# Earlier side pieces, reordered products and low parts made by adding transfers, ahead of one gate of a decoder layer

## The chip, the cores and the metric

The kernel runs on one core of a Trainium2 chip. The metric is device time in microseconds (us), the median of several runs. TensorE (PE) multiplies matrices, VectorE (DVE) and ScalarE (ACT) work elementwise, GpSimd (POOL) and SyncE (SP) here only issue DMA transfers. All data are float32; matrix products take operands in the type float32r.

## The reference

One layer of a hybrid decoder over 512 tokens of width 1024. Only the following parts matter here (`h` is the normalised and modulated input, 512 x 1024; the three gates and all mixer inputs are columns of `h @ w_in`):

```python
y_ssd  = (normed y) @ w_ssd_out          # y from the state-space mixer
y_attn = o @ w_attn_out
y_pool = (_multi_scale_pool(u, w_pool_mix) * pool_scale) @ w_pool_out
g_ssd, g_attn, g_pool = split(sigmoid(gates))
x = x + g1 * ((g_ssd * y_ssd + g_attn * y_attn + g_pool * y_pool) @ w_out)
...
x = x + g2 * (square(relu(h2 @ w_ff1)) @ w_ff2)
```

`_multi_scale_pool` takes running means of `u` over windows of 2, 4, 8 and 16 tokens, subtracts `u`, and multiplies each of the four groups of 256 columns by a 256 x 256 matrix of `w_pool_mix`.

## The kernel before, in words

**Products in three parts.** To keep float32 accuracy each operand is split in a high part (`wh`, `xh`: cast to float32r) and a low part (`wl`, `xl`: the original less the high part). A product is three matmuls (`mm3`, lines L293 to L295): high weights by low input, high by high, low weights by high input.

**Chunks.** Activations lie transposed: 8 tiles of 128 features by 512 tokens (`hh`, `hl` for the high and low part of `h`). A weight matrix is used in chunks of 512 output columns. `gemm_feat` computes one chunk: `wstream` loads its rows in steps of 256 (two tiles, 512 KB, one DMA on SP's queue), `wsplit` casts on ScalarE (`wh`) and subtracts on VectorE (`wl`, L279), and TensorE does 2 x 4 x 3 = 24 matmuls of 128 x 512 per step. A chunk of 1024 rows has four steps. The pool `raws` has four buffers for loaded weights; `wsp` has three for `wh` and three for `wl`, so step n is split when step n-3 has been used.

**Seven products.** Some chunks are computed by `seven_products`, a scheme with seven quarter products in place of eight (168 matmuls of 128 x 256, L811). Four of its weight quarters go in as sums (`N`, and `L` in place; made by VectorE, L793 to L796), three as they are: `a00`, `a01`, `a11`. Four of the products use sums of input tiles, `tq`, which `input_sums` makes once for several chunks, in four pieces (VectorE, L753 to L758, then a split into `txh`, `txl`, `tyh`, `tyl`). The others use the plain `hh`, `hl`. It loads the whole chunk as four DMAs: `rawl`, two tiles into the places L0 and L1, and `raw`, two into `raws`. In the code `a00` comes first, then the two products with `N` (for which `tq` is needed), then `a01`, and so on.

**Side pieces.** Small work of other parts (heads of the state-space mixer, norms, the mixes) is a list `side` of functions. `tick()`, called after each step of a weight stream, takes one piece from the list and issues it behind `edges`, the cast and the subtraction of that step. `rest(n)` puts n empty pieces in the list; `flush()` issues all that are left.

**The region of the change.** In order: the two chunks `pool(0)` and `pool(1)` (`u`, then the windows on VectorE, `pdh` and `pdl`), the gate chunk `gate(GS, 0)` (by `gemm_feat`), the projection `project(a["w_ssd_out"], 8, 0, ...)`, the gate chunk `gate(GS, 1, tq)`, which is the first by `seven_products`, and its projection. Beside these, as side pieces: `mix_weights(n)` loads and splits the mix matrices of two groups into the places L0, N0 (n = 0) or L1, N1 (n = 1); `pool_mix(gi)` does the 12 matmuls of one group (`psmix`), scales the result, splits it (`poolh`, `pooll`) and stores it to DRAM by four POOL transfers (L1146); then the four pieces of `input_sums`. When `pool(0)` begins, seven pieces of the state-space heads are still in the list. They and the pieces of this region are taken in the order in which they were put in, one per step.

**Order and places.** Outside a few hand-ordered parts a scheduler orders the instructions of each engine by priority (`high_priority(offset=AHEAD)` for weights, `SOON` for evacuations) and by when it reckons operands to be ready. Each engine's queue is then worked off in order. 49 blocks of 128 x 512 (`blk`) are given out in turn and taken again when they have been used.

Of the kernel before, what the change touches and what calls it, by code (L numbers as in the profile page):

```python
# [17 lines left out]
P = 128  # L18
# [80 lines left out]
def kernel(ctx: ExitStack, tc: tile.TileContext, a: dict, out: bass.AP, dbg=None):  # L99
# [13 lines left out]
    def uid(s):  # L113
        cnt[0] += 1
        return f"{s}_{cnt[0]}"
# [19 lines left out]
    def blk(name, dt=F32):  # L135
        return sb.take(name, dt)
# [18 lines left out]
    def acc():  # L155
        return psm("acc")
# [114 lines left out]
    def flush():  # L271
        while side:
            side.pop(0)()


    def wsplit(raw, shape):
        wh = wsp.tile(shape, F32R, tag="wh", name=uid("wh"))
        wl = wsp.tile(shape, F32R, tag="wl", name=uid("wl"))
        edges[:] = S.copy(wh, raw), V.tensor_tensor(wl, raw, wh.bitcast(F32), ALU.subtract)  # L279
        return wh, wl  # L280

    def wstream(w, nk, ch, k0=0, ahead=None):
        for kp in range(nk // 2):
            with tc.high_priority(offset=AHEAD if ahead is None else ahead):
                raw = raws.tile([P, 2, T], F32, tag="raw", name=uid("raw"))
                nc.sync.dma_start(raw, w[ch, k0 // 2 + kp])
                wh, wl = wsplit(raw, [P, 2, T])
            for i in range(2):
                yield 2 * kp + i, wh[:, i, :], wl[:, i, :]
            tick()  # L290
# [472 lines left out]

        return tq, [piece(k) for k in range(4)]

    def seven_products(w, ch, xh, xl, tq, last=False):

        L, N, H = [], [], []
        in_b = lambda row, ts: lambda k: (xh[4 * row + k][:, ts], xl[4 * row + k][:, ts])
        in_t = lambda n: lambda k: tuple(t[:, halves[n % 2]] for t in tq[k][n // 2])  # L770
        quarters = lambda t: t.rearrange("p i (n c) -> p (i n) c", n=2)
        lo, hi = ta, tb
        with tc.high_priority(offset=AHEAD):
            for m in range(2):
                L.append(exp.tile([P, 2, T], F32, tag=f"L{m}", name=uid("rawl")))
                H.append(raws.tile([P, 2, T], F32, tag="raw", name=uid("raw")))
                nc.sync.dma_start(L[m], w[ch, m])
                nc.sync.dma_start(H[m], w[ch, 2 + m])

            def parts(srcs):  # L780

                wh = wsp.tile([P, 2, T], F32R, tag="wh", name=uid("wh"))
                wl = wsp.tile([P, 2, T], F32R, tag="wl", name=uid("wl"))
                outs = [(wh, wl)] if len(srcs) == 1 else [(quarters(wh)[:, 2 * m : 2 * m + 2, :], quarters(wl)[:, 2 * m : 2 * m + 2, :]) for m in range(2)]
                for x, (h, l) in zip(srcs, outs):
                    S.copy(h, x)  # L786
                    V.tensor_tensor(l, x, h.bitcast(F32), ALU.subtract)  # L787
                return wh, wl

            a00 = parts([L[m][:, :, lo] for m in range(2)])  # L790
            for m in range(2):
                n = exp.tile([P, 2, T], F32, tag=f"N{m}", name=uid("wsum"))
                V.tensor_tensor(n[:, :, lo], L[m][:, :, hi], H[m][:, :, hi], ALU.add)  # L793
                V.tensor_tensor(L[m][:, :, hi], L[m][:, :, lo], L[m][:, :, hi], ALU.subtract)
                V.tensor_tensor(n[:, :, hi], n[:, :, lo], L[m][:, :, lo], ALU.subtract)
                V.tensor_tensor(L[m][:, :, lo], H[m][:, :, lo], n[:, :, hi], ALU.subtract)  # L796
                N.append(n)

        def pair(p, cols):
            return [tuple(t[:, i, cols] for t in p) for i in range(2)]  # L800

        def quarter(p):
            return [tuple(quarters(t)[:, i, :] for t in p) for i in range(4)]

        def product(ps, k0, ws, b, first=False):
            for k, (wh, wl) in enumerate(ws, k0):
                bh, bl = b(k)
                for j in range(2):
                    o, cs = ps[:, j * 256 : j * 256 + 256], slice(j * P, (j + 1) * P)
                    for n, (x, y) in enumerate(((wh, bl), (wh, bh), (wl, bh))):  # L810
                        mm(o, lhsT=x[:, cs], rhs=y, start=first and k == 0 and j == 0 and n == 0, stop=k == 3 and n == 2, skip_group_check=True)  # L811

        def keep(ps):
            with tc.high_priority(offset=SOON):
                t = blk("keep")
                S.copy(t, ps)
            return t

        def add(j0, ts, x, y):
            with tc.high_priority(offset=SOON):  # L820
                for j in range(2):
                    c = slice(j * 256, j * 256 + 256)
                    V.tensor_tensor(rs[j0 + j][:, ts], x[:, c], y[:, c], ALU.add)
            free(x, y)

        X, Z = acc(), acc()
        product(X, 0, quarter(a00), in_b(0, ta), first=True)
        p1 = keep(X)
        for m in range(2):
            with tc.high_priority(offset=AHEAD):  # L830
                s12 = parts([N[m]])
            product(Z, 2 * m, pair(s12, lo), in_t(0), first=True)
            if m == 1:
                p5 = keep(Z)
            product(X, 2 * m, pair(s12, hi), in_t(1))
            tick()
        u2 = keep(X)
        if last:
            for t, _ in tq:
                free(*t)  # L840
        rs = [blk("r") for _ in range(4)]
        with tc.high_priority(offset=AHEAD):
            a01 = parts([H[m][:, :, lo] for m in range(2)])
        Y = acc()
        product(Y, 0, quarter(a01), in_b(1, ta), first=True)
        add(0, ta, Y, p1)
        for m in range(2):
            with tc.high_priority(offset=AHEAD):
                s43 = parts([L[m]])
            product(X, 2 * m, pair(s43, hi), in_t(2))  # L850
            if m == 1:
                u3 = keep(X)
            product(Z, 2 * m, pair(s43, lo), in_b(1, tb))
            tick()
        add(0, tb, Z, u2)
        add(2, tb, u3, p5)
        with tc.high_priority(offset=AHEAD):
            a11 = parts([H[m][:, :, hi] for m in range(2)])
        product(X, 0, quarter(a11), in_t(3))
        with tc.high_priority(offset=SOON):  # L860
            for j in range(2):
                S.copy(rs[2 + j][:, ta], X[:, j * 256 : j * 256 + 256])
        free(X)
        if last:
            for _, t in tq:
                free(*t)
        return rs
# [4 lines left out]
    def gate(c, ch, tq=None, last=False):  # L872
        if tq is None:
            return evac(gemm_feat(w_in, 8, c + ch, hh, hl), "sg", AF.Sigmoid)
        rs = seven_products(w_in, c + ch, hh, hl, tq, last)
        for r in rs:
            S.activation(r, r, AF.Sigmoid)
        return rs
# [221 lines left out]
    def pool(half):  # L1100
        us = evac(gemm_feat(w_in, 8, U + half, hh, hl), "u")
        for j in range(4):
            gi = 2 * half + j // 2
            u = us[j]
            cur, d = u, 1
            while d < WINDOWS[gi]:
                nx = blk("win")
                V.tensor_copy(nx[:, :d], cur[:, :d])
                V.tensor_tensor(nx[:, d:], cur[:, d:], cur[:, : T - d], ALU.add)
                if cur is not u:  # L1110
                    free(cur)
                cur, d = nx, 2 * d
            V.tensor_tensor(cur[:, : d - 1], cur[:, : d - 1], C("edge")[:, gi * 16 : gi * 16 + d - 1], ALU.mult)
            V.scalar_tensor_tensor(cur, cur, 1.0 / d, u, ALU.mult, ALU.subtract)
            free(u)
            x, y = split(cur, "pd")
            free(cur)
            dh.append(x)
            dl.append(y)
# [41 lines left out]
    def call(f, *args):  # L1161
        side.append(lambda: f(*args))
# [22 lines left out]
    def rest(n):  # L1185
        side.extend([lambda: None] * n)
# [55 lines left out]
    project(a["w_attn_out"], 4, 1, oh, ol, sg, first=True)  # L1242
    show("oT", [h.bitcast(F32) for h in oh + ol])
    tq, sums = input_sums(hh, hl)
    for half in range(2):
        call(mix_weights, half)
        pool(half)
        rest(2)
        call(pool_mix, 2 * half)
        if half == 0:  # L1250
            call(pool_mix, 1)
    side.append(lambda: (pool_mix(3), sums[0]()))
    side.extend(sums[1:])
    sg = gate(GS, 0)
    project(a["w_ssd_out"], 8, 0, yh, yl, sg)
    flush()
    sg = gate(GS, 1, tq)
    project(a["w_ssd_out"], 8, 1, yh, yl, sg)

# [262 lines left out]
```

## Time and profile before

| | |
|---|---|
| median of 3 runs | 1106.65 us (1105.22 to 1106.88) |
| the profiled execution | 1104.65 us |
| its span, first to last instruction | 1102.9 us |
| TensorE busy | 1087.0 us, 99% of the span |
| VectorE busy | 761.6 us, 69% |
| ScalarE busy | 536.9 us, 49% |
| GpSimd busy | 29.2 us, 3% |
| mean granted TensorE clock | 0.995 of full speed |
| DMA traffic | 142.42 MB, mean 129 GB/s |

A row of a group or a tile names the line, the engine, the operation and `out<-in`, then durations in ns; a row of the timeline gives the start and the duration in us, and in square brackets how long the engine was idle before, and what ended that. A row of a stretch gives its length and each engine's busy time, the granted clock, the share of the DMA engines' time, and GB/s. Matmuls overlap in the pipeline, so their durations exceed the distance of their starts.

### The profile page before, as it was taken

What the parts mean: (1) busy time and instruction counts of PE and PEld (TensorE: products, weight loads), DVE (VectorE), ACT (ScalarE), POOL (GpSimd) and SP (SyncE); (2) the same over time, 40 slices, a digit from 0 to 9 for tenths busy, and PEclk for the clock granted to TensorE, in tenths of its full rate; (3) what the DMA queues carried; (4) which work ended last, traced back from release to release, by engine and by line L of the source; (5) the groups of instructions that cost most, each with busy time, mean ns of one, the idle gap of its engine ahead of it and who ended that gap; (6) DMA issues with size and microseconds to landing.
All of it is one profiled execution on the core that took longest, in us unless ns stands there. A gap on an engine that the chain in (4) does not pass through costs nothing.

```text
span 1102.9 us, 15616 instructions
## 1 busy us (share of the span) xinstructions
PE 1087.0 (99%) x6022; PEld 937.8 (85%) x6022; DVE 761.6 (69%) x1441; ACT 536.9 (49%) x877; POOL 29.2 (3%) x58
## 2 busy tenths in 40 slices
PE   8999999999999999999988999999999999999998
PEld 7878888888887888888877899899889989989987
DVE  8955746683777956678777557476797587687664
ACT  8965864643545942835425245363344334335330
POOL 0000000000000000000110200000000000000000
PEclk9999999999999999999998999999999999999999
DMA  9723143555644342223534542560224134133032
GB/s 346 296 96 100 65 162 123 176 169 182 203 151 156 102 134 99 93 77 96 191 114 132 172 155 71 178 229 1 77 58 136 64 108 134 56 116 135 20 115 77
DMA packets 49230, 142.42 MB, mean 129 GB/s; under 512 B 5874, under 2 KB 6642, under 8 KB 49156
## 3 DMA queue, kind: packets, MB, share of 16 engines
q1 hardware_dynamic: 43088, 126.08, 34.5%
q0 software_dynamic: 5344, 14.16, 4.2%
q10 hardware_dynamic: 724, 1.18, 0.3%
q8 instruction: 47, 0.77, 0.3%
q14 instruction: 27, 0.22, 0.1%
HBM read 135.08 MB, written 6.32 MB: 128 GB/s over the span
## 4 chain that ended last, share of the span: by engine, by line
PE 79%; issue 16%; DVE 2%; DMA 1%; POOL 1%; ACT 0%; SPq 0%; POOLq 0%; DVEq 0%; ACTq 0%
PE psacc L293 18%; PE psacc L295 18%; PE psacc L294 18%; PE psacc L811 16%; PE psacc L533 4%; PE psS L612 1%; PE pso L728 1%; PE pso L726 1%; POOL pool L1146 1%; PE psqT L591 0%; PE pskT L596 0%; PE pspT L709 0%; DMA xT<-in_x_dram 0%; DMA pool<-pooll 0%; POOL M L1044 0%
## 5 line engine op out<-in xcount | busy, mean ns | idle before, releaser
L279 DVE TENSOR_TENSOR wl<-raw,wh 128x1024 fp32r<-128x1024 f32 x128 | 156.2, 1221 | 138.3 <-ACT wh L279 132.8
L279 ACT CAST wh<-raw 128x1024 fp32r<-128x1024 f32 x128 | 134.2, 1049 | 208.8 <-PE psacc L294 118.6
L293 PE MATMUL psacc<-hl,wh 128*128 128x512 f32 x320 | 128.8, 403 | 0.2 <-ACT pT L710 0.2
L294 PE MATMUL psacc<-hh,wh 128*128 128x512 f32 x320 | 124.6, 390 | 0.0
L295 PE MATMUL psacc<-hh,wl 128*128 128x512 f32 x320 | 124.5, 390 | 0.0
L293 PE MATMUL psacc<-al,wh 128*128 128x512 f32 (+1 forms) x260 | 100.4, 386 | 0.0
L294 PE MATMUL psacc<-ah,wh 128*128 128x512 f32 (+1 forms) x260 | 100.4, 386 | 0.0
L295 PE MATMUL psacc<-ah,wl 128*128 128x512 f32 (+1 forms) x260 | 100.3, 386 | 0.0
L293 PE MATMUL psacc<-wl,rh 128*128 128x512 f32 x192 | 77.4, 403 | 0.0
L295 PE MATMUL psacc<-wh,rl 128*128 128x512 f32 x192 | 75.2, 392 | 0.0
L294 PE MATMUL psacc<-wh,rh 128*128 128x512 f32 x192 | 75.2, 392 | 0.0
L293 PEld LDWEIGHTS psacc<-hl,wh 128*128 128x128 f32 x320 | 60.1, 188 | 13.4 <-issue 1.2
L294 PEld LDWEIGHTS psacc<-hh,wh 128*128 128x128 f32 x320 | 60.2, 188 | 13.3 <-issue 1.4
L295 PEld LDWEIGHTS psacc<-hh,wl 128*128 128x128 f32 x320 | 60.1, 188 | 12.9
L787 DVE TENSOR_TENSOR wl<-rawl,wh 128x512 fp32r<-128x512 f32 (+1 forms) x36 | 33.7, 954 | 35.6 <-ACT wh L786 35.6
L1441 DVE SCALAR_TENSOR_TENSOR xr<-psacc,modv,xr 128x512 f32<-128x512 f32 (+1 forms) x65 | 44.7, 738 | 18.7 <-PE psacc L295 18.7
L295 PEld LDWEIGHTS psacc<-ah,wl 128*128 128x128 f32 x260 | 48.8, 188 | 9.9
L293 PEld LDWEIGHTS psacc<-al,wh 128*128 128x128 f32 x260 | 48.9, 188 | 9.7
L294 PEld LDWEIGHTS psacc<-ah,wh 128*128 128x128 f32 x260 | 48.9, 188 | 9.6
L786 ACT CAST wh<-rawl 128x512 fp32r<-128x512 f32 (+1 forms) x36 | 29.2, 833 | 51.3 <-PE psacc L294 28.7
L786 ACT CAST wh<-wsum 128x1024 fp32r<-128x1024 f32 x18 | 19.0, 1053 | 72.0 <-PE psacc L294 69.5
L811 PE MATMUL psacc<-txl,wh 128*128 128x256 f32 x144 | 42.0, 292 | 4.4 <-DVE txl L321 4.4
(423 smaller groups left out, 2746.5 us busy)
## 6 DMA issues: line engine op xcount, KB each, us to landing
raw<-in_w_in_dram SPq DMA_DIRECT2D x74, 512.0 KB, 3.6
raw<-in_w_ff_dram SPq DMA_DIRECT2D x52, 512.0 KB, 3.8
wa<-in_w_ada_dram SPq DMA_DIRECT2D x64, 256.0 KB, 3.5
wada<-in_w_ada_dram SPq DMA_DIRECT2D x14, 512.0 KB, 7.8
rawl<-in_w_ff_dram SPq DMA_DIRECT2D x12, 512.0 KB, 3.5
wst<-in_w_in_dram SPq DMA_DIRECT2D x16, 256.0 KB, 7.8
M<-prow POOLq DMA_DIRECT2D x16, 256.0 KB, 3.7
raw<-in_w_ssd_out_dram SPq DMA_DIRECT2D x8, 512.0 KB, 3.6
```

What stands on the lines that cost most here:

```text
L279: edges[:] = S.copy(wh, raw), V.tensor_tensor(wl, raw, wh.bitcast(F32), ALU.subtract)
L293: mm(ps, lhsT=wh, rhs=xl, start=first, stop=False)
L294: mm(ps, lhsT=wh, rhs=xh, start=False, stop=False)
L295: mm(ps, lhsT=wl, rhs=xh, start=False, stop=last)
L533: mm(ps[j], lhsT=t[:, j, :], rhs=w, start=first, stop=last)
L612: mm(so[b], lhsT=qT[:, b * P : (b + 1) * P], rhs=kT[:, (b + 1) * P - n : (b + 1) * P], start=True, stop=True)
L726: mm(od, lhsT=vs[kb][:, hs], rhs=pT[b // 2][:, cs : cs + P], start=(b == 0), stop=False, skip_group_check=True)
L728: mm(ov[:, b, :], lhsT=vs[b][:, hs], rhs=pT[0][:, b * P : (b + 1) * P], start=False, stop=(gi == 2 and b == 3), skip_group_check=True)
L786: S.copy(h, x)
L787: V.tensor_tensor(l, x, h.bitcast(F32), ALU.subtract)
L811: mm(o, lhsT=x[:, cs], rhs=y, start=first and k == 0 and j == 0 and n == 0, stop=k == 3 and n == 2, skip_group_check=True)
L1441: V.scalar_tensor_tensor(xT[d][:, ts], p[:, : ts.stop - ts.start], modv[:, 3, d : d + 1], xT[d][:, ts], ALU.mult, ALU.add)
```

## The change

Three edits, all in the region above.

1. The pieces: no `rest(2)`. `pool(0)` and `pool(1)` follow each other with only `mix_weights(0)` put in between; the four mixes go in the list ahead of `gate(GS, 0)`, the second with `mix_weights(1)`; the four input sums behind them, each a piece of its own.
2. In `gate(GS, 1)` the product of `a01` with the plain input (`first_quarter`) is done behind that of `a00`, ahead of the products with `N` and `tq`.
3. In the twelve steps of `pool(1)`, `gate(GS, 0)` and the first projection, `wl` is made another way: ScalarE writes minus `wh` into it, and a transfer issued by GpSimd adds the weights from DRAM to it. VectorE's subtraction falls away.

```diff
+    def wsplit_add(raw, src):
+
+        wh = wsp.tile([P, 2, T], F32R, tag="wh", name=uid("wh"))
+        wl = wsp.tile([P, 2, T], F32R, tag="wl", name=uid("wl"))
+        S.copy(wh, raw)
+        edges[0] = S.mul(wl, wh.bitcast(F32), -1.0)
+        nc.gpsimd.dma_start(wl, src, accum_op=ALU.add)
+        return wh, wl
+
...
-                wh, wl = wsplit(raw, [P, 2, T])
+                if st.get("adds"):
+                    wh, wl = wsplit_add(raw, w[ch, k0 // 2 + kp])
+                else:
+                    wh, wl = wsplit(raw, [P, 2, T])
...
-    def seven_products(w, ch, xh, xl, tq, last=False):
+    def seven_products(w, ch, xh, xl, tq, last=False, sums_late=False):
...
         X, Z = acc(), acc()
         product(X, 0, quarter(a00), in_b(0, ta), first=True)
         p1 = keep(X)
+
+        def first_quarter():
+            rs.extend(blk("r") for _ in range(4))
+            with tc.high_priority(offset=AHEAD):
+                a01 = parts([H[m][:, :, lo] for m in range(2)])
+            Y = acc()
+            product(Y, 0, quarter(a01), in_b(1, ta), first=True)
+            add(0, ta, Y, p1)
+
+        rs = []
+        if sums_late:
+            first_quarter()
         for m in range(2):
...
-        rs = [blk("r") for _ in range(4)]
-        with tc.high_priority(offset=AHEAD):
-            a01 = parts([H[m][:, :, lo] for m in range(2)])
-        Y = acc()
-        product(Y, 0, quarter(a01), in_b(1, ta), first=True)
-        add(0, ta, Y, p1)
+        if not sums_late:
+            first_quarter()
...
-        rs = seven_products(w_in, c + ch, hh, hl, tq, last)
+        rs = seven_products(w_in, c + ch, hh, hl, tq, last, c == GS)
...
     tq, sums = input_sums(hh, hl)
-    for half in range(2):
-        call(mix_weights, half)
-        pool(half)
-        rest(2)
-        call(pool_mix, 2 * half)
-        if half == 0:
-            call(pool_mix, 1)
-    side.append(lambda: (pool_mix(3), sums[0]()))
-    side.extend(sums[1:])
+
+    pool(0)
+    call(mix_weights, 0)
+    st["adds"] = True
+    pool(1)
+    call(pool_mix, 0)
+    side.append(lambda: (mix_weights(1), pool_mix(1)))
+    call(pool_mix, 2)
+    call(pool_mix, 3)
+    side.extend(sums)
     sg = gate(GS, 0)
     project(a["w_ssd_out"], 8, 0, yh, yl, sg)
     flush()
+    st["adds"] = False
     sg = gate(GS, 1, tq)
     project(a["w_ssd_out"], 8, 1, yh, yl, sg)
```

## The prediction

> **What bounds the kernel now.** I read the page first, then the waits of TensorE over the whole run, then stretches of the region that the change touches, then single instructions there.
>
> ```profile
> span 1102.9 us, 15616 instructions
> PE 1087.0 (99%) x6022; PEld 937.8 (85%) x6022; DVE 761.6 (69%) x1441; ACT 536.9 (49%) x877; POOL 29.2 (3%) x58
> PE psacc L811 <- DVE txl L321: 4.4, 2, 3.0
> PE psacc L811 <- ACT wh L786: 3.5, 2, 3.0
> PE psacc L811 <- DVE wl L787: 1.1, 2, 0.7
> ```
>
> The first two lines are the page's head: TensorE (PE) is busy for 1087.0 of 1102.9 us, so nothing that another engine does costs time unless TensorE waits for it. The last three are its largest waits in the whole run: total, times, longest. All stand at L811, the products of `seven_products`, and together they are 9.0 us. The question is whether they lie at one place.
>
> ```profile
> core 0: us, PE busy (x) PEld busy (x) DVE busy (x) ACT busy (x) POOL busy (x), PEclk, DMA share, GB/s
> 493.80:515.60 21.80, 21.80 (x105) 18.12 (x104) 18.64 (x40) 11.97 (x17) 0.00 (x0) 1.00 0.37 117
> 515.60:542.72 27.12, 27.12 (x122) 22.44 (x121) 23.11 (x49) 13.36 (x19) 2.17 (x4) 1.00 0.43 137
> 542.72:569.85 27.13, 26.99 (x119) 22.04 (x118) 17.63 (x28) 6.79 (x10) 4.43 (x9) 1.00 0.32 117
> 569.85:604.43 34.58, 25.52 (x170) 23.92 (x169) 26.12 (x46) 15.94 (x24) 4.69 (x9) 0.85 0.47 152
> 626.38:646.70 20.32, 20.32 (x169) 20.20 (x169) 13.62 (x20) 10.57 (x16) 2.11 (x4) 1.00 0.60 183
> ...
> 569.85:575.15 5.30, 2.33 (x19) 2.10 (x18) 3.60 (x7) 1.81 (x3) 2.02 (x4) 1.00 0.96 316
> 575.15:585.67 10.52, 8.87 (x38) 8.08 (x38) 10.41 (x20) 3.91 (x6) 0.00 (x0) 0.52 0.11 42
> 585.67:604.43 18.76, 14.31 (x115) 13.74 (x115) 12.10 (x20) 10.21 (x15) 2.67 (x5) 1.00 0.54 168
> ```
>
> These are stretches with TensorE's busy time after the comma. The first three are, roughly, `pool(1)`, the first gate chunk with two pool mixes, and the first projection with the other two: TensorE has no hole. The fourth is the first gate made by `seven_products`: 34.58 us. The fifth is the next such gate, with as many products (168 matmuls of L811): 20.32 us. So the first one loses 34.58 - 20.32 = 14.26 us, of which 34.58 - 25.52 = 9.06 is idle. The other 5.2 are the clock: between 575.15 and 585.67 it was granted at 0.52 of full speed.
>
> Why it is late:
>
> ```profile
> 569.84 21.19 SPq L777 DMA_DIRECT2D rawl<-in_w_in_dram  x3
> 573.83 1.29 DVE L753 TENSOR_TENSOR tq<-hh,hl 128x512 f32<-128x512 f32 x2 [1.69 <-DMA pool<-pooll]
> 574.48 0.62 ACT L786 CAST wh<-rawl 128x512 fp32r<-128x512 f32 x1 [3.21 <-DMA rawl<-in_w_in_dram]
> 575.15 0.38 PE L811 MATMUL psacc<-hl,wh 128*128 128x256 f32 x1 [2.97 <-ACT wh L786]
> ...
> 589.35 0.39 PE L811 MATMUL psacc<-txl,wh 128*128 128x256 f32 x1 [1.44 <-DVE txl L321]
> 594.04 0.39 PE L811 MATMUL psacc<-txl,wh 128*128 128x256 f32 x1 [3.00 <-DVE txl L321]
> ...
> L295 PE MATMUL psmix<-pdh,wmN x16: 389/389/390, 531.8 to 569.6; 128*128 128x512 f32 x16
> L321 DVE TENSOR_TENSOR txl<-tq,txh x8: 679/682/691, 570.1 to 819.4; 128x512 fp32r<-128x512 f32 x8
> ```
>
> Two chains, both from the last pool mix. Its matmuls end at 569.6; its weights lie in the place L1 that the second `rawl` load needs, so that load is issued only at 569.84, lands, is cast, and TensorE gets it at 575.15 (2.97 idle). And the input sums (`tq`, `txl`) stand behind the mixes in the list of side pieces, and take blocks that the mixes' stores to DRAM set free (the 573.83 row): the last two come 1.44 and 3.00 us late.
>
> **The change part by part.**
>
> *No empty pieces, mixes ahead of the sums.* A piece is issued at each of a chunk's four steps. Before, seven pieces are left over when `pool(0)` starts; with one taken per step, the mixes stand at gate steps 3 and 4 and projection step 4, and the rest, the sums among it, is flushed behind it. After, `pool(1)` starts with three left and one added, uses up four, and the four mixes fall on the four gate steps, the four sums on the projection's four. TensorE's work is the same, so the gate by seven products still starts at about 569.85 if nothing stalls. The last mix moves ahead by the projection:
>
> ```profile
> 511.63 0.39 PE L293 MATMUL psacc<-hl,wh 128*128 128x512 f32 x1
> 511.86 0.39 PE L294 MATMUL psacc<-hh,wh 128*128 128x512 f32 x1
> ```
>
> Starts are 0.227 us apart, so a step of 24 matmuls is 5.44 us and a chunk of four is 21.8. The last mix ends near 548 instead of 569.6; the `rawl` load then lands some 17 us ahead of its use, and the 2.97 is gone. The last `txl` started about 24 us after the last mix (594.04 less 0.7 less 569.6); at the same lag it starts at 571.7 and ends at 572.4. With 48 matmuls of the plain input ahead at 0.12 (20.32/168), sums 0 and 1 are needed at 569.85 + 5.8 = 575.6 and sums 2 and 3, 24 matmuls later, at 578.5: 3 to 6 us of slack. That the mixes read `pool(1)`'s windows earlier costs nothing while the windows are done: the last mix runs at 545, and the last `pdl` was
>
> ```profile
> 537.78 0.69 DVE L321 TENSOR_TENSOR pdl<-win,pdh 128x512 fp32r<-128x512 f32 x1 [0.74 <-ACT pdh L320]
> ...
> L1130 DVE TENSOR_TENSOR wmN<-wmix,wmL x2: 1214/1220/1226, 500.1 to 530.1; 128x1024 fp32r<-128x1024 f32 x2
> L1146 POOL DMA_DIRECT2D pool<-poolh x8: 539/539/544, 533.9 to 571.1; - x8
> ```
>
> What moves with the pieces: the second mix weights' two loads on SP, their cast and their subtraction (the row at 530.1; they are wanted from gate step 3 on, near 532, so a late one would hold that mix, and TensorE behind it, for 1 or 2 us at most), and sixteen POOL stores of 0.54 us, off the path unless they hold up an add (below).
>
> *Plain products first.* The matmuls are the same. TensorE had already done the 24 of `a01` ahead of most sums in the old order:
>
> ```profile
> 579.42 0.58 PE L811 MATMUL psacc<-hl,wh 128*128 128x256 f32 x1 [0.54 <-ACT wh L786]
> ...
> 583.96 0.41 PE L811 MATMUL psacc<-hh,wl 128*128 128x256 f32 x1
> ```
>
> The 24 products in these rows have `hl` and `hh`, the plain input, and the two late rows of `txl` above (589.35, 594.04) come behind. So alone I give it 0; at best it saves the wait that 24 x 0.12 = 2.9 us cover, at worst it takes a bank earlier, which no row shows to be short.
>
> *Low parts by adding transfers.* Twelve steps, in `pool(1)`, the gate and the projection. VectorE loses 12 subtractions and ScalarE gets 12 multiplies beside its casts; POOL gets 12 issues, and the DMA engines read 6.3 MB again.
>
> ```profile
> L279 DVE TENSOR_TENSOR wl<-raw,wh 128x1024 fp32r<-128x1024 f32 x128 | 156.2, 1221 | 138.3 <-ACT wh L279 132.8
> L279 ACT CAST wh<-raw 128x1024 fp32r<-128x1024 f32 x128 | 134.2, 1049 | 208.8 <-PE psacc L294 118.6
> 548.09 1.05 ACT L279 CAST wh<-raw 128x1024 fp32r<-128x1024 f32 x1 [4.00 <-PE psacc L294]
> L1263 POOL DMA_DIRECT2D poolh<-pool x8: 527/534/550, 592.8 to 630.4; - x8
> raw<-in_w_in_dram SPq DMA_DIRECT2D x74, 512.0 KB, 3.6
> wada<-in_w_ada_dram SPq DMA_DIRECT2D x14, 512.0 KB, 7.8
> wmix<-in_w_pool_mix_dram SPq DMA_DIRECT2D x4, 256.0 KB, 2.8
> poolh<-pool POOLq DMA_DIRECT2D x8, 256.0 KB, 3.3
> ```
>
> VectorE: 12 x 1.22 = 14.6 us less. It is 23.11 of 27.12 busy in the gate stretch and gets the sums earlier there, so this is what lets the lag above hold; in itself it moves TensorE by 0. ScalarE: 12 x 1.05 = 12.6 us more, in stretches where it is busy 11.97, 13.36 and 6.79 us: hidden, but in series with the cast. The price is the wait for `wl`. There are three buffers: ScalarE casts step n's weights when step n-3 is over (the 548.09 row waits for TensorE), and they are needed two steps later, 10.9 us, the low part 0.45 (two matmuls) later still. Before, cast and subtraction take 1.05 + 1.22. After, cast 1.05 + multiply 1.05 + issue 0.53 + about 0.4 for the semaphores leave 8.3 us for the transfer L, issue to landing. If L is longer, each third step is late by L - 8.3 (three buffers rotate), so twelve steps cost 4 x (L - 8.3).
>
> No row shows an adding transfer. From below: no better than the plain load of 512 KB, 3.6 us, so a cost of 0; a gain is excluded, since TensorE has no hole there. From above: 512 KB while the queues were full took 7.8, and if the addition doubles all of it, 15.6: 4 x 7.3 = 29 us. I take it nearer the light rows, since the DMA share here is 0.32 to 0.43: 2.8 for 256 KB and 3.6 for 512 say 0.8 per 256 KB; POOL's 3.3 for 256 KB plus 0.8 is 4.1, and if the addition moves the bytes twice, 1.6 more: L = 5.7 us, an estimate. Cost 0, with 2.6 us to spare. POOL's order can eat that: four stores per mix, 0.54 each, ahead of an add take 2.2.
>
> *What is late next.* In the new gate stage, the sums. I leave half of the 4.4 us that TensorE waited for `txl`: 2.2, between 0 (the second such gate) and 4.4.
>
> **Sum.** The profiled execution took 1104.65 us, 1.75 beyond its span; the median of the runs is 1106.65, 2.0 above it. Stage 34.58 to 20.32 + 2.2 = 22.5: 12.06 less. Profiled 1092.6; as a median 1094.6 us.
>
> The clock is part of it. The idle stretch before 575.15 was followed by 10.5 us at 0.52; the 3.00 us before 594.04 was not (clock 1.00 in that stretch). The Trainium skill, "TensorE: Matmul & The Clock Gate", Part 1, has the rate halved after an idle window of about 3.4 us, counted in free-running windows; both rows are compatible with it. By that rule a left-over stall of 2.2 costs no clock, and one above 3 may cost 5 more.
>
> **The rivals.**
>
> *The adds land late, and it is slower.* Place: `pool(1)`, the gate and the projection, TensorE idle ahead of L295. For it: nothing in the trace proves L, POOL's queue is in order, and its stores wait for mixes that wait for TensorE. Against it: the rows of loads at this DMA share. It eats the gain at 12.06/4 = 3.0 beyond 8.3, L = 11.3 us. Halfway between 11.3 and 15.6, at 13.4, it costs 20.4: 1115.0 us.
>
> The Trainium skill's page "Collectives: The Full Stack", Part 3, in its section on the bandwidth ceiling, speaks for this rival: an addition in the DMA path needs two source reads on the same ring and ran at half the rate of a copy. By it the row of 3.6 gives 7.2 and the sum stays at 1094.6; the row of 7.8 gives 15.6 and 1094.6 + 29.2 = 1123.8. No row here shows which.
>
> *The sums are late all the same.* They need blocks that the stores set free, and the stores now stand between adds that wait for a multiply that waits for a TensorE step. Two steps, 10.9 us, less the slack of 3 to 6 leave 5 to 8 us of the 14.3: about 1100.5 us. For it: the 573.83 row. Against it: the mixes come 22 us earlier, which holds four steps.
>
> *The adds eat it up*, L near 11: within 0.2% (2.2 us, about what the measurement can tell from no change) of 1106.65.
>
> **How the numbers follow.** Forecast (the stage closes to within 0 to 5 us, adds hidden): 0.56, range 1091.8 to 1097.5. Sums late: 0.17. Eaten up: 0.08. Slower: 0.19. Faster: 0.56 + 0.17 = 0.73, less 0.03 for late sums together with somewhat late adds: 0.70. Same: 0.10, with 0.02 of that; slower 0.20, with 0.01. Range: from the whole stage recovered, 1106.65 - 14.26 = 1092.4, less 0.6 for the spread of the runs, 1091.8, to 1109, which leaves out most of the slower case and takes in a small overrun of the adds (L = 11.9).
>
> **What would show it.** The first gate by seven products: near 22 us, clock 1.00, `rawl` issued about 20 us ahead of it, no wait for `txl` over 2 us. Adds: landing 4 to 8 us after issue, and no TensorE wait for them in the three chunks. VectorE's busy total down by 14.6, ScalarE's up by 12.6. Wrong if TensorE waits at L295 for a DMA, or if `pool` stores are held up in POOL's queue by several steps and the sums with them.

## The result, and the profile after

The changed kernel takes 1096.26 us (1096.12 to 1096.79) where the kernel before took 1105.93 (1104.63 to 1106.88) on the same chip, four runs of each: ratio 0.9914, 95% interval 0.9897 to 0.9931. The forecast was 1094.6. The profiled execution took 1096.12 us.

The page's head and two DMA queues, then the waits of TensorE over the whole run, all of the kernel after (line numbers are 12 higher than before up to `seven_products`, and 20 higher for the mixes: L305 is the first matmul of `mm3`, L823 the products of `seven_products`, L1161 and L1162 the scalings of a mix, L1166 its stores; L281 and L282 are the new multiply and add). A queue's row gives packets, MB, and its packets' time as a share of 16 DMA engines' span.

```profile
span 1094.3 us, 15638 instructions
PE 1083.6 (99%) x6022; PEld 935.3 (85%) x6022; DVE 748.4 (68%) x1429; ACT 547.8 (50%) x889; POOL 39.8 (4%) x70
q1 hardware_dynamic: 43088, 126.08, 34.5%
q0 software_dynamic: 7072, 20.45, 7.7%
PE psacc L305 <- DVE pooll L1162: 4.0, 1, 4.0
PE pssx L423 <- DVE sq L432: 1.5, 1, 1.5
```

No wait at L823 is left. The longest is a new one: TensorE waits 4.0 us at an ordinary product for `pooll`, the low part of a pool mix's result. It stands in the first projection. The windows of the kernel after (columns as in the prediction's):

```profile
core 0: us, PE busy (x) PEld busy (x) DVE busy (x) ACT busy (x) POOL busy (x), PEclk, DMA share, GB/s
484.00:545.00 61.00, 61.00 (x292) 50.40 (x291) 45.26 (x105) 35.82 (x49) 12.76 (x18) 1.00 0.86 214
545.00:574.00 29.00, 24.95 (x103) 20.16 (x102) 22.18 (x43) 15.04 (x23) 5.56 (x9) 0.94 0.57 167
550.20:554.40 4.20, 0.15 (x2) 0.03 (x1) 4.07 (x9) 4.20 (x8) 1.46 (x2) 1.00 0.85 272
554.40:558.60 4.20, 4.20 (x12) 3.30 (x13) 4.12 (x7) 0.00 (x0) 1.60 (x3) 0.61 0.99 286
575.59:595.92 20.33, 20.33 (x170) 20.20 (x168) 13.69 (x20) 10.63 (x14) 2.67 (x5) 1.00 0.53 156
```

The last row is the first gate by seven products: 20.33 us where it took 34.58, with no hole and a clock of 1.00. The second row holds the projection ahead of it, from 547.90 to 575.59: 27.7 us where four steps take 21.8. Of the 5.9 lost, 4.05 are the wait (third row), and the rest goes with the clock, granted at 0.61 behind it (fourth row). So -14.25 and +5.9 make -8.35 of the span's -8.6. The first row has the third novelty: from 484 to 545 the DMA engines are busy for 0.86 of the time.

How the new wait comes about is read from single rows of the timeline:

```profile
534.41 0.54 POOL L1166 DMA_DIRECT2D pool<-pooll  x1
543.82 0.69 DVE L765 TENSOR_TENSOR tq<-hh,hl 128x512 f32<-128x512 f32 x1 [5.00 <-DMA pool<-pooll]
546.33 0.62 ACT L332 CAST txh<-tq 128x512 fp32r<-128x512 f32 x1 [5.71 <-DVE tq L768]
547.90 0.39 PE L305 MATMUL psacc<-ynl,wh 128*128 128x512 f32 x1
548.27 0.60 ACT L344 ACTIVATE sg<-psacc 128x512 f32<-128x512 f32 x1
550.23 0.69 DVE L765 TENSOR_TENSOR tq<-hh,hl 128x512 f32<-128x512 f32 x1 [1.73 <-DMA pool<-pooll]
552.09 1.28 ACT L1161 ACTIVATE poolh<-psmix,vec 128x512 fp32r<-128x512 f32 x2
553.58 1.40 DVE L1162 SCALAR_TENSOR_TENSOR pooll<-psmix,vec,poolh 128x512 fp32r<-128x512 f32 x2
554.37 0.50 PE L305 MATMUL psacc<-ynl,wh 128*128 128x512 f32 x1 [4.05 <-DVE pooll L1162]
...
575.59 0.28 PE L823 MATMUL psacc<-hl,wh 128*128 128x256 f32 x1
```

The projection starts at 547.90 and the gate by seven products at 575.59. The mix's store to DRAM is issued at 534.41. VectorE's first input sum takes the block that this store sets free, and stands idle for 5.00 us until it has landed, at 543.82: 9.4 us after its issue. ScalarE, in order, idles 5.71 at the cast of that sum; behind it stand the gate's sigmoids (548.27 and on) with a table load of 1.28 us, one of the new multiplies (1.06 us at 550.19), and the scaling of the last mix (552.09). VectorE has a second sum that waits for a store, 1.73 us at 550.23, ahead of its `pooll`. That scaling and `pooll` empty the mix's PSUM banks, and TensorE waits for one. DMA landings: the row of L282, the adds, and that of L1166, the mixes' stores:

```profile
DMA to landing us min/median/max: 5.1/5.8/8.3
DMA to landing us min/median/max: 2.3/5.3/9.4
```

The adds land after 5.8 us in the median, and TensorE waits for none of them. The stores beside them take up to 9.4. So no late add holds TensorE. The reading of these rows is that the adds load the DMA engines and make other transfers late: this is what the experiments had to show or to refute.

### The profile page after: what moved, and what is told of

Read it like the earlier page. It is cut to its first block, busy times and chain, and to the rows that moved or that the text cites. A ratio compares the mean times of both kernels' runs of the same rounds, so it can differ in the third digit from the quotient of the medians.

```text
span 1094.3 us, 15638 instructions
## 1 busy us (share of the span) xinstructions
PE 1083.6 (99%) x6022; PEld 935.3 (85%) x6022; DVE 748.4 (68%) x1429; ACT 547.8 (50%) x889; POOL 39.8 (4%) x70
## 3 DMA queue, kind: packets, MB, share of 16 engines
q1 hardware_dynamic: 43088, 126.08, 34.5%
## 4 chain that ended last, share of the span: by engine, by line
PE 95%; DVE 2%; DMA 2%; ACT 0%; issue 0%; POOL 0%; SPq 0%; DVEq 0%; ACTq 0%; POOLq 0%
PE psacc L305 22%; PE psacc L307 22%; PE psacc L306 22%; PE psacc L823 17%; PE psacc L545 4%; PE psS L624 1%; DMA pool<-pooll 1%; PE psy L1084 1%; PE pso L740 1%; PE psyo L1092 1%; PE pso L738 1%; PE psqT L603 0%; PE pskT L608 0%; PE psst L1043 0%; DMA xT<-in_x_dram 0%; PE pspT L721 0%
## 5 line engine op out<-in xcount | busy, mean ns | idle before, releaser
L288 DVE TENSOR_TENSOR wl<-raw,wh 128x1024 fp32r<-128x1024 f32 x116 | 141.6, 1222 | 128.8 <-ACT wh L288 121.0
L288 ACT CAST wh<-raw 128x1024 fp32r<-128x1024 f32 x116 | 121.5, 1048 | 188.1 <-PE psacc L306 108.3
L305 PE MATMUL psacc<-hl,wh 128*128 128x512 f32 x320 | 128.8, 403 | 0.2 <-ACT pT L722 0.2
L307 PE MATMUL psacc<-hh,wl 128*128 128x512 f32 x320 | 124.7, 390 | 0.0
L306 PE MATMUL psacc<-hh,wh 128*128 128x512 f32 x320 | 124.6, 389 | 0.0
L306 PE MATMUL psacc<-ah,wh 128*128 128x512 f32 (+1 forms) x260 | 100.4, 386 | 0.0
L305 PE MATMUL psacc<-al,wh 128*128 128x512 f32 (+1 forms) x260 | 100.4, 386 | 0.0
L307 PE MATMUL psacc<-ah,wl 128*128 128x512 f32 (+1 forms) x260 | 100.3, 386 | 0.0
L305 PE MATMUL psacc<-wl,rh 128*128 128x512 f32 x192 | 77.3, 403 | 0.0
L307 PE MATMUL psacc<-wh,rl 128*128 128x512 f32 x192 | 75.2, 392 | 0.0
L306 PE MATMUL psacc<-wh,rh 128*128 128x512 f32 x192 | 75.2, 391 | 0.0
L305 PEld LDWEIGHTS psacc<-hl,wh 128*128 128x128 f32 x320 | 60.1, 188 | 13.5 <-issue 1.2
L306 PEld LDWEIGHTS psacc<-hh,wh 128*128 128x128 f32 x320 | 60.2, 188 | 13.3 <-issue 1.4
L307 PEld LDWEIGHTS psacc<-hh,wl 128*128 128x128 f32 x320 | 60.1, 188 | 12.8
L307 PEld LDWEIGHTS psacc<-ah,wl 128*128 128x128 f32 x260 | 48.8, 188 | 9.9
L305 PEld LDWEIGHTS psacc<-al,wh 128*128 128x128 f32 x260 | 48.9, 188 | 9.7
L306 PEld LDWEIGHTS psacc<-ah,wh 128*128 128x128 f32 x260 | 48.9, 188 | 9.6
L305 PEld LDWEIGHTS psacc<-wl,rh 128*128 128x128 f32 x192 | 36.1, 188 | 7.7 <-ACT qT L604 0.5
```

What stands on the lines that cost most here:

```text
L305: mm(ps, lhsT=wh, rhs=xl, start=first, stop=False)
L306: mm(ps, lhsT=wh, rhs=xh, start=False, stop=False)
L307: mm(ps, lhsT=wl, rhs=xh, start=False, stop=last)
```

## The experiments

All ratios are to the kernel before in runs on the same chip, five rounds each. The experiments ran on several chips, so medians of different experiments are compared by their ratios first. Waits are read from one profiled execution each.

### The three edits apart

Without the adds (`e1_no_adds`):

```diff
-    st["adds"] = True
```

> The changed kernel with the low parts of the three chunks subtracted on VectorE again, no adding transfers; order of pieces and products as changed. Theory A (the order of the pieces gives most of the gain, the adds only relieve VectorE): slower than the changed kernel's 1096.3 us but faster than before, 1097 to 1102, with VectorE 14.6 us busier and the sums later. Rival B (the relief of VectorE gives the gain): 1104 to 1107. Rival C (the adds fill the DMA queues, so that the stores of the mixes land late, and blocks, sums and one PSUM bank with them: the 4.0 us stall in the first projection is theirs): that stall goes and it is faster than the changed kernel, 1091 to 1094.

Measured: 1091.10 us, 0.9871 (0.9856 to 0.9886). The waits of TensorE and two windows:

```profile
PE psacc L305 <- DVE pooll L1162: 1.8, 1, 1.8
484.00:545.00 61.00, 61.00 (x291) 50.43 (x290) 55.60 (x116) 30.18 (x42) 6.47 (x12) 1.00 0.43 151
545.00:574.00 29.00, 27.17 (x129) 22.49 (x129) 24.20 (x46) 12.21 (x20) 2.16 (x4) 1.00 0.30 102
```

The wait falls from 4.0 to 1.8, the clock stays at 1.00, the DMA share is half, and the mixes' stores land after 6.7 us at most:

```profile
DMA to landing us min/median/max: 2.3/5.1/6.7
```

The adds cost about 5 us, as rival C had it; VectorE, 55.60 of 61 us busy without them, keeps up. The theory that the adds relieve it to some use (1097 to 1102 without them) is wrong.

The adds with the old pieces and the old order of products (`e2_adds_only`, from the kernel before, with `wsplit_add` and its call as in the change):

```diff
     for half in range(2):
         call(mix_weights, half)
+        st["adds"] = half == 1
         pool(half)
...
     flush()
+    st["adds"] = False
```

> The kernel before with adding transfers in the three chunks and nothing else: empty pieces and product order as before. Theory A: the second rawl load still waits for the last mix and the sums still stand behind it, so the stage of the first gate by seven products stays near 34 us: 1104 to 1107 us. Rival B: the relief of VectorE gives the gain: 1096 to 1100.

Measured: 1105.03 us, 0.9997 (0.9988 to 1.0005).

```profile
PE psacc L823 <- DVE txl L333: 4.5, 2, 3.0
PE psacc L823 <- ACT wh L798: 3.7, 2, 3.1
484.00:545.00 61.00, 61.00 (x291) 50.30 (x290) 42.34 (x98) 39.92 (x53) 11.99 (x17) 1.00 0.84 201
```

The old waits stand unchanged, with the DMA share at 0.84: by themselves the adds neither help nor hurt. The stores land late there too (up to 7.9 us after issue, 5.4 before), and a sum on VectorE waits 1.79 us for one at 553.38; but the last mix comes only at the end of the projection, and TensorE waits for no `pooll`.

The new kernel with the old order of products (`e3_sums_first`):

```diff
-        rs = seven_products(w_in, c + ch, hh, hl, tq, last, c == GS)
+        rs = seven_products(w_in, c + ch, hh, hl, tq, last)
```

> The changed kernel with the old order of products (N and tq ahead of a01). Theory A: the last txl ends at 566.4 in the changed kernel and with the old order is wanted at about 573.5 + 2.9, so nothing waits: 1096.3 us within 0.2%. Rival D (the plain products first are needed): a stall in the gate stage of up to 2.9 us, 1098 to 1100.

Measured: 1096.53 us, 0.9924 (0.9912 to 0.9937): no difference from the change. The plain products first are worth nothing, since the sums are ready. In the kernel after, the last mix's matmuls end at 548.1, the last `txl` starts at 565.71, ten us ahead of the gate, and the last `tyl` at 568.72:

```profile
L307 PE MATMUL psmix<-pdh,wmN x16: 389/389/389, 521.2 to 547.7; 128*128 128x512 f32 x16
565.71 0.69 DVE L333 TENSOR_TENSOR txl<-tq,txh 128x512 fp32r<-128x512 f32 x1
```

The pieces alone, without adds and in the old order of products (`e11_pieces_only`, from the kernel before):

```diff
-    for half in range(2):
-        call(mix_weights, half)
...
+    pool(0)
+    call(mix_weights, 0)
+    pool(1)
+    call(pool_mix, 0)
+    side.append(lambda: (mix_weights(1), pool_mix(1)))
+    call(pool_mix, 2)
+    call(pool_mix, 3)
+    side.extend(sums)
```

> The kernel before with the new order of the side pieces and nothing else: no adds, old order of products. Theory A (the pieces give the whole gain): 1091.1 us within 0.2%, as with the plain products first. Rival D (the plain products are needed): a stall at the gate by seven products, 1092.5 to 1095 us.

Measured: 1091.57 us, 0.9880 (0.9865 to 0.9896). TensorE's wait in the projection is shorter here than in `e1_no_adds`, which has the same pieces and subtractions and differs in the order of products alone:

```profile
PE psacc L305 <- DVE pooll L1162: 0.6, 1, 0.6
```

So 0.6 here and 1.8 there: differences of about 1 us between the waits of single profiles prove nothing. The medians in us:

| | subtractions | adds |
|---|---|---|
| old pieces, old order of products | 1105 to 1106 (before) | 1105.03 |
| new pieces, old order of products | 1091.57 | 1096.53 |
| new pieces, new order of products | 1091.10 | 1096.26 (after) |

The pieces are the whole gain, 13.75 us (1105.32 less 1091.57 on the same chip); with the new pieces the order of products is nothing in either column (with the old ones it was not run); the adds cost 5 us, but only beside the new pieces.

### Which part of an add costs

The transfer without the add's place in the kernel (`e10_spare_adds`): the subtractions stay, and POOL issues twelve transfers of the same 512 KB in the same steps, from `wl` to a DRAM array that nobody reads. The first stores, the others add.

```diff
+        if st.get("more"):
+            first = "spare" not in st
+            if first:
+                st["spare"] = dp.tile([P, 2, T], F32, name="spare")
+            nc.gpsimd.dma_start(st["spare"], wl.bitcast(F32), **({} if first else {"accum_op": ALU.add}))
...
-    st["adds"] = True
+    st["more"] = True
```

> The kernel of e1 (subtractions on VectorE, 1091.1 us) plus twelve transfers of 512 KB, issued by GpSimd at each step of the three chunks, which add wl to a DRAM array that nobody reads (the first one stores). Nothing waits for them except the next of them and the reuse of the wl buffer. Rival G2 (the load on the DMA engines makes the changed kernel's 5 us): 1094 to 1097 us, stores of the mixes landing up to 9 us after issue, the stall back at about 4 us. Theory J (it is the place of the sums in VectorE's queue): 1090.5 to 1092 us.

Measured: 1097.74 us, 0.9932 (0.9920 to 0.9945). TensorE's longest wait, two windows, the landing of the mixes' stores, and three rows of the timeline (line numbers are 5 higher here):

```profile
PE psacc L310 <- DVE pooll L1167: 4.9, 1, 4.9
484.00:545.00 61.00, 61.00 (x291) 50.38 (x290) 53.37 (x111) 30.94 (x43) 13.79 (x21) 1.00 0.85 210
545.00:574.00 29.00, 24.06 (x97) 19.35 (x96) 21.45 (x40) 9.55 (x17) 4.24 (x7) 0.88 0.65 176
DMA to landing us min/median/max: 2.4/8.3/9.1
546.65 1.28 ACT L1166 ACTIVATE poolh<-psmix,vec 128x512 fp32r<-128x512 f32 x2
550.24 0.69 DVE L770 TENSOR_TENSOR tq<-hh,hl 128x512 f32<-128x512 f32 x1 [1.71 <-DMA pool<-pooll]
552.66 1.41 DVE L1167 SCALAR_TENSOR_TENSOR pooll<-psmix,vec,poolh 128x512 fp32r<-128x512 f32 x2
```

No product takes its operand from these transfers, and the profile shows one wait for them, 2.0 us of POOL. VectorE and ScalarE do what they do in `e1_no_adds`, and yet the wait is back (4.9 for 1.8), at the same place, with the same late stores. The transfers cost it. ScalarE's part of the chain is not needed for that: here it scales the last mix at 546.65, before any late cast, and it is VectorE alone that comes late, with a sum that waits for a store at 550.24 ahead of `pooll` at 552.66. What stays open is how the cost divides between the transfers' bytes, POOL's twelve issues and their being additions: a variant with twelve plain transfers wasn't run.

### Five attempts to break the chain

The scaling of the mix ahead in priority (`e4_mix_soon`):

```diff
+            with tc.high_priority(offset=SOON):
                 S.activation(x, ps, AF.Copy, ...)
                 V.scalar_tensor_tensor(y, ps, ...)
```

> The changed kernel, the two scalings of each mix (ScalarE and VectorE, which set its PSUM bank free) at the priority SOON, ahead of the input sums in the engines' queues. Theory E (the 4.0 us stall at 550 in the first projection is a PSUM bank that the last mix holds because its scaling stands behind the sums and the gate's sigmoids): the stall and the slow clock behind it go, 1090 to 1093 us. Rival F (it is an adding transfer that lands late): 1096.3 us within 0.2%, the stall as it was.

Measured: 1095.88 us, 0.9917 (0.9904 to 0.9931), and TensorE still waits 4.2. A row of its timeline:

```profile
546.76 0.62 ACT L332 CAST txh<-tq 128x512 fp32r<-128x512 f32 x1 [6.62 <-DVE tq L768]
```

The scaling is now ahead of the last two sigmoids (551.56), but ScalarE stands just as long at the cast of the sum, and that cast is still ahead of it. The time is the one of rival F, the mechanism is not: TensorE waits for `pooll`, and for no add.

An empty piece between the mixes and the sums (`e5_rest`):

```diff
     call(pool_mix, 3)
+    rest(1)
     side.extend(sums)
```

> The changed kernel with one empty piece between the mixes and the input sums. Theory G (with the adds the mixes' stores land up to 9.4 us after issue; the first sum, early in VectorE's queue, waits 5.0 us for a block that such a store sets free, ScalarE waits 5.7 us for that sum ahead of the gate's sigmoids, and the last mix's PSUM bank comes free late): with the sums a step later the chain breaks, the 4.0 us stall and the slow clock go: 1090 to 1093 us. Rival H (the adds themselves, by ScalarE's 12.6 us more, hold the bank): 1096.3 within 0.2%.

Measured: 1096.36 us, 0.9919 (0.9905 to 0.9933), wait 4.7. With the adds, one empty piece is not enough: the first sum still idles 3.36 us for a store and starts at 544.27, where it started at 543.82 in the change. The time fits rival H, but `e10_spare_adds` has the wait without ScalarE's multiplies. Without the adds (`e6_no_adds_rest`):

```diff
-    st["adds"] = True
...
     call(pool_mix, 3)
+    rest(1)
     side.extend(sums)
```

> The same empty piece, and no adding transfers. Theory G: the 1.8 us stall that is left without the adds goes: 1089 to 1090.5 us. Rival H: 1091.1 within 0.2%. Should VectorE, with the subtractions back, be too late with sums that start a step later, a stall at the gate by seven products takes it to 1092 to 1096.

Measured: 1090.28 us, 0.9863 (0.9850 to 0.9877).

```profile
span 1088.8 us, 15621 instructions
545.00:574.00 29.00, 29.00 (x144) 24.33 (x143) 28.68 (x53) 13.62 (x21) 2.70 (x5) 1.00 0.35 114
```

TensorE has no hole in the projection. This is the fastest version that was run: it beats the kernel before, and the change too: the interval of the change begins at 0.9897, this one ends at 0.9877. From `e1_no_adds` (0.9856 to 0.9886) and `e11_pieces_only` (0.9865 to 0.9896) its time can't be told apart, and it fits theory G and rival H alike; with 0.6 us of waiting in `e11_pieces_only`, the empty piece is not shown to be what closed the hole.

The mixes' stores on SyncE's queue in place of POOL's (`e7_stores_sp`):

```diff
-                nc.gpsimd.dma_start(l[-1], t.bitcast(F32))
+                nc.sync.dma_start(l[-1], t.bitcast(F32))
```

> The changed kernel with the sixteen stores of the mixes issued from SP in place of GpSimd, so that they do not stand behind adding transfers in one queue. Theory G1 (the stores land late because of the order in GpSimd's queue): they land in 2 to 5 us, the wait for a block and the stall go, 1090 to 1093 us. Rival G2 (the DMA engines are simply full, share 0.91 in the gate stretch): landing stays at up to 9 us, 1096.3 within 0.3%. Against both: SP waits for the mixes ahead of weight loads, which may make it slower.

Measured: 1095.25 us, 0.9910 (0.9896 to 0.9923). TensorE's wait, and the landing of the stores:

```profile
PE psacc L305 <- DVE pooll L1162: 3.0, 1, 3.0
DMA to landing us min/median/max: 2.8/5.4/8.5
```

The wait is 1.0 shorter, no more than single profiles differ, and the stores land up to 8.5 us after their issue from a queue that holds no add. POOL's order is at most a part of it.

The adds only in `pool(1)` and the gate, not in the projection (`e8_adds_two`):

```diff
     sg = gate(GS, 0)
+    st["adds"] = False
     project(a["w_ssd_out"], 8, 0, yh, yl, sg)
```

> The changed kernel with adding transfers in pool(1) and the gate chunk alone; the projection's low parts are subtracted again. Theory G: the four adds of the projection are issued from 531 on, beside the stores of the mixes; without them the stores land earlier and most of the stall goes: 1091 to 1093.5 us. Rival H': the adds ahead of 531 did it, 1095 to 1097.

Measured: 1095.41 us (five runs, 1092.24 to 1095.78), 0.9905 (0.9890 to 0.9920). The profiled execution is one of the shorter ones, 1093.73 us:

```profile
551.02 0.50 PE L305 MATMUL psacc<-ynl,wh 128*128 128x512 f32 x1 [2.09 <-DVE pooll L1162]
551.00:553.00 2.00, 1.98 (x7) 1.59 (x8) 1.23 (x2) 0.00 (x0) 1.08 (x2) 0.81 0.72 270
553.00:554.00 1.00, 1.00 (x3) 0.75 (x3) 0.00 (x0) 0.00 (x0) 0.00 (x0) 0.50 1.08 430
```

The wait is halved, and still the clock falls behind it. The median is in the range of rival H', but the five runs spread over 3.5 us: the shortest, 1092.24, kept a mean clock of 1.000, the other four show 0.997 or 0.998. Only one was profiled, so the experiment does not tell how much of the cost the four adds of the projection carry.

### An anchor for the side pieces

A side piece goes behind two `edges`, the cast and the subtraction of a step; with adds there is no subtraction, so the second edge stays an old one, and a piece has ScalarE's multiply alone. A one-column VectorE copy into a small tile of its own put the second edge back (`e9_anchor`):

```diff
-        edges[0] = S.mul(wl, wh.bitcast(F32), -1.0)
+        edges[:] = S.mul(wl, wh.bitcast(F32), -1.0), V.tensor_copy(small([P, 1], "mark"), wh[:, 0, 0:1].bitcast(F32))
```

> The changed kernel, where each adding step also does a one-column VectorE copy from wh (under 0.2 us), so that the side pieces are again placed behind this step on VectorE as well (with adds alone the anchor there is an old subtraction). Theory J (without that anchor the sums stand too early in VectorE's queue, and wait there for blocks): the waits for pool<-pooll on VectorE and the 4.0 us stall go, 1090 to 1092.5 us. Rival G2 (the full DMA engines bring the blocks late whatever the place in the queue): 1094 to 1097 us.

Measured: 1101.16 us, 0.9964 (0.9953 to 0.9976), though TensorE's wait was only 3.5. The loss lies elsewhere. Groups of TensorE's instructions by shape (line, names, count, busy us, mean ns), of `e9_anchor`:

```profile
L306 PE MATMUL psacc<-hh,wh 128*128 128x512 f32 x320 | 126.6, 396 | 0.0
L306 PE MATMUL psacc<-ah,wh 128*128 128x512 f32 x252 | 98.1, 389 | 0.0
```

The products with `hh` and `hl` at L305 to L307, 960 in all, take some 6 ns more than in the change (126.6 us for 124.6 in the group of L306); those with `ah` don't. By the code the new tile may move tiles that are placed behind it. So once more, with the copy going into a column of the tile `gap`, which was there already and unused (`e12_anchor`):

```diff
-    small([P, 704], "gap")
+    gap = small([P, 704], "gap")
...
-        edges[0] = S.mul(wl, wh.bitcast(F32), -1.0)
+        edges[:] = S.mul(wl, wh.bitcast(F32), -1.0), V.tensor_copy(gap[:, 0:1], wh[:, 0, 0:1].bitcast(F32))
```

> As e9, but the one-column copy goes to a column of a tile that is there already and not used (gap), so that no tile moves. In e9 the matmuls with hl and hh took 396 ns in place of 390, in all 960 of them, which is worth about 5 us by itself. Theory K (the moved places of the tiles made these matmuls slower): here they take 390 ns again, and the rest is as in e9: stall 3.5 to 4 us, 1094 to 1097 us, so the anchor alone does not help (G2 holds against J). Rival L (the extra VectorE copy of a column of wh itself slows the matmuls): 396 ns, near 1101 us. Theory J: 390 ns, no stall, 1090 to 1092.5 us.

Measured: 1094.72 us (1092.50 to 1096.44), 0.9899 (0.9882 to 0.9915).

```profile
L306 PE MATMUL psacc<-hh,wh 128*128 128x512 f32 x320 | 124.6, 390 | 0.0
PE psacc L305 <- DVE pooll L1162: 4.3, 1, 4.3
```

The products are as fast as ever, and the wait is as long as in the change. The anchor is no remedy, and the 5 to 6 us of `e9_anchor` (960 products by 6 ns) came with the new tile and not with the copy. That the tile's place does it is the likely reading; no view shows the places.

## Why the prediction was right, and where it was not

**What bounds the kernel, and the pieces: right.** The stage was to fall from 34.58 us; it fell to 20.33 with clock 1.00, and `e11_pieces_only` has all of the gain from the pieces alone. One reading was loose: the three waits shown are not TensorE's three largest, since one of 1.4 us at L411 (`pssx`) stands among them. It is at another place and still there after (1.5 at L423), so nothing hangs on it. The last mix was to end near 548 and ended at 548.1; the last `rawl` load was to be issued about 20 us ahead of the gate and was issued at 550.21, 25 us ahead; the sums' lag behind it, taken as 24 us, is 565.71 - 548.1 = 17.6.

**Plain products first, 0: right** beside the new pieces, by `e3_sums_first` against the change and `e1_no_adds` against `e11_pieces_only`.

**What is late next, 2.2 us at the new gate: wrong.** There is nothing late at the gate. What is late is 25 us ahead of it, in the projection, and not a sum but what stands behind a sum on VectorE and ScalarE.

**The adds, 0: this is the term that was mis-sized, by about 5 us.** The transfer itself came out as estimated, L = 5.7 against a measured 5.8 in the median and 8.3 at most, which is the budget; VectorE's total fell by 13.2 (14.6 forecast) and ScalarE's rose by 10.9 (12.6). The step that failed priced an add only by the wait for its own result. The argument "the DMA share here is 0.32 to 0.43" was taken from the kernel without adds, while the adds raise that share to 0.86. The two queues' rows give the size. POOL's queue took 4.2% of 1102.9 us before and 7.7% of 1094.3 after:

```profile
q0 software_dynamic: 5344, 14.16, 4.2%
```

That is 84.3 - 46.3 = 38 us more of all 16 engines for twelve adds, 3.2 us each (at most, since the stores beside them were slower too); SyncE's loads, 34.5% for 126.08 MB, come to 1.57 us for 512 KB. By this reckoning an add occupies the engines about twice as long as a load. The Trainium skill, "Collectives: The Full Stack", Part 3, says of an addition in the DMA path, there of ReduceScatter against AllGather, that it needs two source reads and runs at half the rate of a copy; the trace agrees, 3.2 against 1.57, for an add issued by a kernel. The prediction used that rule for the landing time of the add alone, where it led to 7.2 or 15.6 us; the measured 5.8 is below both. Its price was the share of the engines.

**The rivals.** "The adds land late" did not happen: TensorE waits for none. "The sums are late all the same" named the mechanism that is there, blocks that stores set free, but at the gate and through POOL's queue; it acts through the landing of the stores, in the projection, and costs 5.9 of the 14.3, in its range of 5 to 8. (Its price of 1100.5 us is the upper end of that range, 1092.4 + 8; the whole of it is 1097.4 to 1100.4.) That the forecast's time came within 2 us is therefore in part luck: the gate gave all of its 14.25 back, 2.2 more than was counted on, and a term priced at nothing took about 5. The forecast's 12.05 us came out as 9.7 by the medians.

**The clock.** After 4.05 us idle it was granted at 0.61, at a cost of 1.85, as the prediction had it for a stall above 3 us ("5 more" was too much). That a stall of 2.2 costs no clock does not hold: 2.09 us idle in `e8_adds_two` were followed by a stretch at 0.50, while before the change 3.00 us were followed by 1.00. The Trainium skill, "TensorE: Matmul & The Clock Gate", Part 1, has an idle window of about 3.4 us ahead of the lower clock; the 3.00 agree with it and the 2.09 do not, and the measurement decides: here a stall shorter than that window cost the clock.

Shown by the experiments: the pieces are the gain, the adds' transfers are the cost, and only beside the new pieces. Read from the profile, and not shown by an experiment that removes it: the chain from a late store by its block to a sum, from there to `pooll` (in the change by ScalarE's cast and scaling too) and the bank. The attempts at single links (priority, queue, an empty piece, an anchor) left at least 3.0 of the wait.

## What to carry to other kernels

A transfer is not free because its own result comes in time: multiply the engines' time that it takes by the number of transfers, add that to the share of the stretch it falls in, and ask which other transfer there has someone waiting for it. When a change has several edits, fill the table of them: here one was worth 13.75 us, one nothing, and one took 5 back, but only in company. An engine that works in order should not get a piece whose operand waits for a store ahead of work that empties a PSUM bank; this last is read from the profile here, and the attempts to put it right beside the adds failed.

## What was not expected of the hardware

- Placing: with one more tile of one column, 960 products with `hl` and `hh` took some 6 ns more (396 in place of 390), 5 to 6 us in all; with the column in an existing tile it was gone. The cause is not shown.
- The clock: 2.09 us idle were followed by a granted 0.50, 3.00 us in another run by 1.00.
- An adding transfer of 512 KB took about 3.2 us of all DMA engines where a load takes 1.57, and POOL's issue of it is the longer one too:

```profile
L282 POOL DMA_DIRECT2D wl<-in_w_in_dram x8: 857/862/892, 477.2 to 523.5; - x8
```

against 0.54 us for a plain store in the rows above.
